# Softmax denominators inverted before they are spread, and one subtraction moved to VectorE

## Chip, core and metric

The kernel runs on one core of a Trainium2 chip. The metric is device time in microseconds (us) of one execution. The engines are TensorE (PE, its weight loads are shown as PEld), VectorE (DVE), ScalarE (ACT), GpSimd (POOL) and SyncE (SP), which issues the DMAs.

## What is computed

A stack of transformer layers over 256 latent and 256 context tokens of 1024 features, all in float32. Four places matter here, all of them softmax attention:

- two layers of the first block, each with 8 query heads of 64 features (grouped, 2 key heads), over 512 keys for a latent token and 256 for a context token;
- a causal attention of 16 heads ("moba"), and a causal attention of 16 heads with compressed keys and queries ("mla"), both over 256 tokens.

```python
s = jnp.einsum("bqhd,bkhd->bhqk", q, k) * scale
p = jax.nn.softmax(s, axis=-1)
out = jnp.einsum("bhqk,bkhd->bqhd", p, v)
```

Between and behind the two causal attentions stand two feed-forward stages (2816 hidden features) with a short convolution, and each attention is followed by an output projection `w_o` of 1024 x 1024.

## The kernel before, in words

**Float32 products in three parts.** Each operand of a large product is split in a rounded part (hi, a cast on ACT) and the rest (lo, `src - hi`). `split` (L130) does this: `S.copy(hi, src)` on ACT and the subtraction on VectorE, unless its last argument names another engine. PE then does hi\*hi, lo\*hi and hi\*lo (`mm3`, L105). Weights come by DMA into `st` (4 buffers), are split into `wh` and `wl` (5 buffers each) and are read by PE; some of the `wl` are made by POOL.

**Softmax without a division of the weights.** For each head PE makes the scores, VectorE takes the maximum, ACT the exponential with the row sum as a by-product (a column of `dn`), PE transposes the weights, ACT or VectorE copies them out of PSUM (`PT`), and PE multiplies them with the values, feature-major, into a bank `pv`. What is still missing is the division by the row sum. The sums are columns (a token is a partition), the values stand as rows (a token is a column), so the inverses must be turned: `inv_rows` (L290) makes from 4 or 8 columns of sums a tile with each inverse 64 times side by side, PE transposes that tile into a bank `tr`, ACT copies the bank to SBUF, and VectorE multiplies `pv` with it.

**Where it is called.** `attend` (L757) calls it for 4 heads at a time, 8 times in the first layer and 4 times in the second; the result goes to `qo` (L800, L801). `out_heads` (L1041) calls it for 8 columns (4 heads by 2 tiles of queries), 4 times in moba and 4 times in mla: the copy on ACT (L1046), the product on VectorE (L1047), and then `split` of the product into `moh`/`mol` or `loh`/`lol`, with the low part on POOL (L1048). These are the operands of the output projection `w_o_proj` (L1050), whose sums go to `h` on VectorE (L1060) and on into the next norm (L982, L983). The tile with the spread inverses is called `t` in `attend` and `rr` in `out_heads`, where it has one buffer.

**Order.** The steps are written in the order of `PLAN` (L46). From it a planner makes one instruction order for each engine before the program runs: it goes through the program with durations that it estimates itself and lets each engine take the foremost instruction that is ready. Each engine then works through its list in that order, whatever the real durations are, and waits at semaphores. `tr`, `sc`, `acc` and `pv` are PSUM banks, two of each.

Of the kernel before, what the change touches and what calls it, by code (L numbers as in the profile page):

```python
# [16 lines left out]
D = 1024  # L17
# [22 lines left out]
# shift 8, scale 8, gate 8  # L40
# [4 lines left out]
# orders of the steps whose results meet only at the end (see the tables `steps`)  # L45
# [11 lines left out]
# pieces of weights whose low parts are worked out by GpSimd (see the keys given to `fetch`)  # L57
# [5 lines left out]
# tile 0, 1: latent tokens; 2, 3: context tokens  # L63
# [5 lines left out]
def tile_two_blocks(ctx: ExitStack, tc: tile.TileContext, A, out, dbg=None):  # L69
# [42 lines left out]
    def stream(pieces, ncol, tiles, sh, sl, tags):  # L112
        """tokens of `tiles` @ a chunk of weights, two k at a time; returns a bank per tile"""
        ps = {t: bank(tag) for t, tag in zip(tiles, tags)}
        for i, w in enumerate(pieces):
            for t in tiles:
                stream_on(ps[t], i, w, ncol, t, sh, sl)
        return ps
# [46 lines left out]
    msk0 = consts.tile([128, 2, 128], F32, name="c_masks")      # 0 / NEG : free > partition, free < partition  # L165
    consts = first.enter_context(tc.tile_pool(name="consts1", bufs=1, side="right", reuse_waits="tile"))

    def rsqrt_into(dst, ss, mean_scale, eps, tmp):
        # dst = (ss * mean_scale + eps) ** -0.5
        n = dst.shape[-1]  # L170
        V.tensor_scalar(tmp, ss, mean_scale, eps, op0=OP.mult, op1=OP.add)
        G.tensor_tensor(dst, tmp, nhalf[:, :n], op=OP.pow)

    # ------------------------------------------------------------------ first block
# [9 lines left out]
    # 512 features of silu(c) @ w_ada + b_ada -> mod[feature, 24, (lat, ctx)]  # L184
    # j < 4: scales of tiles 2j, 2j + 1 of the features and their shifts; then the gates
    def ada_mm(ps, i, st):
        # four quarters of the sum, each in its own columns of the array: they run side by side
        for u in range(2):
            k = 2 * i + u
            r = slice(k % 4 * 32, k % 4 * 32 + 32)  # L190
            mm(ps[r, :], s32[:, k, :], st[u] if type(st) is list else st[:, u * 512:(u + 1) * 512], k < 4, k >= 4)
# [25 lines left out]
    bada = const("b_ada")       # [128, l, 24]  # L217
# [15 lines left out]
    gsec = base.tile([128, 6, 8], F32, name="c_g_sec")      # g_final, norm_mix 0, 1, norm_ffn 0, 1, norm_final  # L233

    def late_consts():
        nc.sync.dma_start(gsec, A["g_sec"])
        late["tri"] = const("tri")          # [128, 2, 128] inclusive prefix / suffix
        late["ropeq"] = const("rope_lat")   # [128, 2 tiles, 2 (cos, sin), 64]
        late["bg"] = const("b_gates")       # [128, l, 16]
        late["gh"] = const("g_head")        # [128, l, 2]  # L240
        late["ends"] = const("ends")        # [128, 2] one in the last / first row
        nc.sync.dma_start(msk0, A["masks"])
        mskp = consts.tile([128, 2, 128], F32, name="mskp")
        G.tensor_scalar(mskp[:, 0], msk0[:, 1], -1.0, None, op0=OP.mult)
        G.tensor_scalar(mskp[:, 1], msk0[:, 0], -1.0, None, op0=OP.mult)
        late["mskp"] = mskp

    class Squares:
        """sum over the features of squares, a tile of 128 features at a time; a column of sums for each tile of tokens"""
# [14 lines left out]
        def add(self, ap, scale=1.0):  # L264
# [10 lines left out]
            if self.k == KT - 1:        # all but the last tile: ahead of it  # L275
                self.ps = bank("tr")
                self.head = self.small("sqh")
                V.tensor_scalar(self.head, self.columns(self.acc, 0), 1.0 / D, self.eps, op0=OP.mult, op1=OP.add)

        def mean(self, dst):  # L280
            """mean of the squares + eps"""
            V.scalar_tensor_tensor(dst, self.columns(self.last, 1), 1.0 / D, self.head, op0=OP.mult, op1=OP.add)
# [7 lines left out]
    def inv_rows(rr, cols):  # L290
        """columns of heads -> rows of 1 / x, a pair of heads in the two halves of the partitions, a pair after the other"""
        n = cols.shape[-1]
        rr = rr[:, :n * 64].rearrange("p (a b) -> p a b", b=64)
        V.reciprocal(rr, cols.unsqueeze(2).to_broadcast([128, n, 64]))  # L294
# [11 lines left out]
    mod_rows = {}       # what is left of the next layer's shifts, scales and gates, and behind which tile  # L306

    def first_layer(l, ncx, x, rc):
        """ncx: context tokens are updated (layer 0) or only read (layer 1)"""
# [8 lines left out]
        # ---- norm  # L318
# [8 lines left out]
        def normed(k, t, r=None):  # L327
# [3 lines left out]
            # the first tile by halves: the products wait for it  # L331
# [12 lines left out]
        gqk = sb.tile([128, 2, 2, 64], F32, name="c_g_qk")      # (q, k), (straight, swapped)  # L344
# [11 lines left out]
        if l == 0:  # L356
            # the first products follow the shifts and scales, two tiles of the features at a time
            def ada_tiles(q):
                """tiles that are not in use yet"""
# [75 lines left out]
        # tables with the gains of q and k folded in  # L435
# [7 lines left out]
        # ---- token-major projections  # L443
# [21 lines left out]
        def rope(dst, src, tab, nh, t, e1=V, e2=V):  # L465
            """dst, src [128, nh, 64]"""
# [11 lines left out]
        # chunk 1: v of the recurrent branch, k and v of the attention  # L478
# [27 lines left out]
        # chunk 3: q of the attention  # L506
# [24 lines left out]
        # chunk 0: k of the recurrent branch and its gates  # L531
# [14 lines left out]
        def gate_stats():  # L546
# [11 lines left out]
            # cumulative sums, their ends (on all partitions and as rows)  # L558
# [45 lines left out]
            V.tensor_tensor(ex[:, 0], mp, Mc, op=OP.subtract)      # inter  # L604
            V.tensor_tensor(ex[:, 1], mp, Me, op=OP.subtract)      # decay of the state
            V.tensor_tensor(ex[:, 2], R, Me, op=OP.subtract)       # weight of a key in the state
# [4 lines left out]
        # chunk 2: q of the recurrent branch, v of the gated mlp  # L611
# [26 lines left out]
        # ---- feature-major gates  # L638
        # a a b b b b c c: the products with the gates land here too
# [17 lines left out]
        # ---- recurrent branch  # L657
# [8 lines left out]
        def scores(c):  # L666
            """heads 0, 2 in one bank, 1, 3 in the other: row tiles of the array run side by side"""
# [6 lines left out]
        HP = [0, 2, 1, 3]       # place of a head in ag  # L674
# [81 lines left out]
        # ---- attention of one tile of queries  # L756
        obs, att = {}, {}  # L757

        def attend(t, i):
            """pair i of the heads"""  # L760
# [4 lines left out]
            if i == 0:  # L765
                # a head: its half holds hi of q, the other half lo
# [26 lines left out]
            # two heads side by side in the columns of the array  # L793
# [15 lines left out]
        def gates(i, q):  # L809
# [3 lines left out]
            if i >= 4:      # bz  # L813
                silu2(gate[:, 2 + (i - 4) * 2 + q, :], ps)
            elif q == 0:    # co; au
# [5 lines left out]
            else:           # cz; az  # L821
# [7 lines left out]
        # gated mlp  # L829
# [20 lines left out]
        # the branches, and products that need none of them in between  # L850
# [14 lines left out]
        if ncx:  # L865
            # what is left of the next layer's shifts, scales and gates
# [33 lines left out]
        if ncx:  # L900
            # they are worked out while the norm is on its way
# [20 lines left out]
        # the next norm: (r^2 * mean((x g)^2) + eps) ** -0.5  # L922
# [15 lines left out]
    def gelu2(dst, ps, tmp):  # L938
        """2 * tanh-gelu(ps); dst and tmp in SBUF"""
# [11 lines left out]
    # ------------------------------------------------------------------ second block  # L951
    consts = ctx.enter_context(tc.tile_pool(name="consts2", bufs=1, reuse_waits="tile"))
    rope2 = const("rope2")      # [128, 2 tiles, (cos, sin), 64]
    rope3 = const("rope3")      # [128, 2 tiles, (cos, sin), 32]
    gqn = const("g_lora")       # [128, 5]: q_norm 3, kv_norm 2
    cw = const("conv")          # [128, l, 22, 4]: taps 0..2, bias
# [9 lines left out]
    class Norm:  # L966
        """next norm of h: hi and lo of h * gain and the sum of squares, as the tiles of h come in"""
# [32 lines left out]
    def scores_of(qT, kT, *heads):  # L1000
        """of heads in different rows of the array: they run side by side"""
# [7 lines left out]
    def weights_of(sb, ps, hd, dn, scale, bufs):  # L1009
        """transposed softmax numerators of a head: [keys, (tile 0, keys 0), (tile 1, keys 0), (tile 1, keys 1)]"""  # L1010
        d0 = hd // 2 * 4 + hd % 2       # pairs of heads, tiles of queries, heads
# [18 lines left out]
    def values_of(PTs, va, g0):  # L1030
        """four heads of P @ v, feature-major: pairs of heads, side by side in the columns of the array"""
# [9 lines left out]
    def out_heads(sb, po, dn, oh, ol, g):  # L1041
        """normalised, hi and lo"""
# [5 lines left out]
        split(oh[:, 2 * g:2 * g + 2, :], ol[:, 2 * g:2 * g + 2, :], o, G)  # L1048
# [95 lines left out]
    def mla(nrm):  # L1144
# [4 lines left out]
        # down projections: 384 of q, then 256 of kv and 32 of the shared key  # L1149
# [10 lines left out]
        def lora_rstd(ps, n, t, dst):  # L1160
            # dst = r * (r^2 * mean(ps^2) + eps) ** -0.5
# [52 lines left out]
        # keys, feature-major  # L1214
# [154 lines left out]
# ---------------------------------------------------------------------- host: layout only  # L1369
def _fp(a):  # L1370
    """[1024, n] -> [128, 8, n]: features on the partitions"""
    return a.reshape(-1, 128, a.shape[-1]).transpose(1, 0, 2)


def _kpack(w):
    """[K, n] -> [128, K/128 * n]"""
    k, n = w.shape
    return w.reshape(k // 128, 128, n).transpose(1, 0, 2).reshape(128, -1)


def _blocks(w, bw=128):
    """[K, N] -> [N/bw, 128, K/128 * bw]"""
# [4 lines left out]
def _pairs(b):  # L1387
    """[2n, 128, m] -> [n, 128, 2m]"""
# [3 lines left out]
def _constants():  # L1392
# [8 lines left out]
    # 2-D rotation of the first block  # L1401
# [78 lines left out]
```

## Time and profile before

| what | before |
| --- | --- |
| time, median of 3 runs | 1162.22 us (1160.79 to 1164.43) |
| span of the profiled execution | 1164.8 us |
| PE busy | 1110.9 us, 95% of the span |
| DVE busy | 765.8 us, 66% |
| ACT busy | 596.9 us, 51% |
| POOL busy | 311.7 us, 27% |
| mean granted TensorE clock | 0.981 |

The profile is that of one execution, and its span, from the first to the last instruction, is 1164.8 us: 0.2% above the median of the timed runs and just above the slowest of them. What lies around the span is not shown. PE works nearly all of the time, so a microsecond of another engine matters where PE waits for it, and only there. The granted clock is 1.0 at 2.4 GHz and 0.5 at 1.2 GHz.

### The profile page before, as it was taken

How to read it: one execution, taken by the hardware profiler on the slowest of the kernel's cores; microseconds unless marked ns; L12 is line 12 of the kernel's file. 1: busy time of each engine (PE TensorE's matmuls, PEld its weight loads, DVE VectorE, ACT ScalarE, POOL GpSimd, SP SyncE). 2: the span in 40 equal slices, each digit the busy share in tenths (PEclk: the TensorE clock that was granted, in tenths of full speed). 3: DMA queues.
4: the chain of work that ended last, by engine and by line, in shares of the span. 5: the costliest groups of instructions: out<-in, count | busy, mean ns of one | idle time of the engine just before them, and what ended most of it. 6: DMA issues, size and time to landing. Idle time of an engine off the chain costs nothing. (4 is left out here: it accounts for less than half of the span.)

```text
span 1164.8 us, 20350 instructions
## 1 busy us (share of the span) xinstructions
PE 1110.9 (95%) x7762; PEld 963.1 (83%) x7762; DVE 765.8 (66%) x1497; ACT 596.9 (51%) x1154; POOL 311.7 (27%) x290
## 2 busy tenths in 40 slices
PE   5899998999899899998999999999999989999997
PEld 2586777687686789887776899999998789999996
DVE  3465555585646666778676777776557877777653
ACT  3435643533434366465456565555447856555541
POOL 3452311131212544424313312221032241222100
PEclk9999998999899899999999999999999999999998
DMA  9523501433742324214443255555644325555561
GB/s 347 200 66 125 177 28 39 142 130 123 259 153 73 101 91 146 74 69 143 162 153 118 82 175 195 184 183 179 182 145 150 135 71 181 185 183 189 175 186 47
DMA packets 52608, 167.29 MB, mean 144 GB/s; under 512 B 6816, under 2 KB 10400, under 8 KB 52512
## 3 DMA queue, kind: packets, MB, share of 16 engines
q1 hardware_dynamic: 52512, 166.01, 42.8%
q8 instruction: 61, 1.00, 0.3%
q14 instruction: 35, 0.29, 0.1%
HBM read 164.41 MB, written 1.05 MB: 142 GB/s over the span
## 5 line engine op out<-in xcount | busy, mean ns | idle before, releaser
L131 ACT CAST wh<-st 128x1024 fp32r<-128x1024 f32 (+4 forms) x272 | 268.5, 992 | 208.9 <-PE acc L100 116.3
L132 DVE TENSOR_TENSOR wl<-st,wh 128x1024 fp32r<-128x1024 f32 (+4 forms) x207 | 244.5, 1183 | 113.3 <-ACT wh L131 108.9
L132 POOL TENSOR_TENSOR wl<-st,wh 128x1024 fp32r<-128x1024 f32 (+4 forms) x65 | 150.9, 2332 | 285.1 <-ACT wh L131 264.5
L100 PE MATMUL acc<-xyh,wh 128*128 128x512 f32 (+1 forms) x320 | 112.5, 352 | 4.3 <-DVE xres L892 2.3
L100 PE MATMUL acc<-xyl,wh 128*128 128x512 f32 (+1 forms) x320 | 111.5, 351 | 2.6 <-DVE xyl L132 2.6
L100 PE MATMUL acc<-xyh,wl 128*128 128x512 f32 (+1 forms) x320 | 111.4, 349 | 0.0
L100 PE MATMUL acc<-wh,xyh 128*128 128x512 f32 (+1 forms) x256 | 97.6, 382 | 6.4 <-DVE t L474 3.3
L100 PE MATMUL sc<-hh,wl 128*128 128x256 f32 x352 | 99.0, 281 | 0.0
L100 PE MATMUL sc<-hl,wh 128*128 128x256 f32 x352 | 99.0, 281 | 0.0
L100 PE MATMUL acc<-hl,wh 128*128 128x256 f32 x352 | 99.0, 281 | 0.0
L100 PE MATMUL acc<-ah,wh 128*128 128x256 f32 x352 | 99.0, 281 | 0.0
L100 PE MATMUL acc<-al,wh 128*128 128x256 f32 x352 | 99.0, 281 | 0.0
L100 PE MATMUL acc<-ah,wl 128*128 128x256 f32 x352 | 98.9, 281 | 0.0
L100 PE MATMUL sc<-hh,wh 128*128 128x256 f32 x352 | 98.9, 281 | 0.0
L100 PE MATMUL acc<-hh,wh 128*128 128x256 f32 x352 | 98.8, 281 | 0.0
L100 PE MATMUL acc<-hh,wl 128*128 128x256 f32 x352 | 98.8, 281 | 0.0
L100 PE MATMUL acc<-wh,xyl 128*128 128x512 f32 (+1 forms) x256 | 96.0, 375 | 0.0
L100 PE MATMUL acc<-wl,xyh 128*128 128x512 f32 (+1 forms) x256 | 95.3, 376 | 0.0
L100 PEld LDWEIGHTS acc<-xyh,wh 128*128 128x128 f32 x320 | 62.2, 194 | 13.5 <-issue 2.8
L100 PEld LDWEIGHTS acc<-xyl,wh 128*128 128x128 f32 x320 | 62.0, 194 | 10.8 <-DVE xyl L132 3.1
L100 PEld LDWEIGHTS acc<-xyh,wl 128*128 128x128 f32 x320 | 62.0, 194 | 7.6
L100 PEld LDWEIGHTS sc<-hl,wh 128*128 128x128 f32 x352 | 66.4, 189 | 0.0
(458 smaller groups left out, 2746.2 us busy)
## 6 DMA issues: line engine op xcount, KB each, us to landing
st<-w_gu SPq DMA_DIRECT2D x88, 512.0 KB, 3.8
st<-w_dn SPq DMA_DIRECT2D x32, 512.0 KB, 3.5
st<-w_in_t SPq DMA_DIRECT2D x24, 512.0 KB, 3.9
st<-w_in_f SPq DMA_DIRECT2D x24, 512.0 KB, 4.7
st<-a_w_qkv SPq DMA_DIRECT2D x24, 512.0 KB, 3.4
st<-w_ada SPq DMA_DIRECT2D x20, 512.0 KB, 3.9
st<-w_out SPq DMA_DIRECT2D x16, 512.0 KB, 4.4
st<-w_dn SPq DMA_DIRECT2D x16, 384.0 KB, 3.3
```

The lines of the kernel that those rows point to most:

```text
L100: last_mm[0] = PE.matmul(o, lhsT, rhs, start=start, stop=stop).ins
L131: S.copy(hi, src)
L132: (lo_eng or V).tensor_tensor(lo, src, hi.bitcast(F32), op=OP.subtract)
```

## The change

`inv_rows` no longer takes 1/x of the spread columns (256 or 512 elements in each partition). It takes 1/x of the 4 or 8 sums in place, and a copy on VectorE spreads the result. And in `out_heads` the low part is subtracted on VectorE, where POOL did it. All else in the diff is removed comments and docstrings.

```diff
     def inv_rows(rr, cols):
...
         n = cols.shape[-1]
         rr = rr[:, :n * 64].rearrange("p (a b) -> p a b", b=64)
-        V.reciprocal(rr, cols.unsqueeze(2).to_broadcast([128, n, 64]))
+        V.reciprocal(cols, cols)
+        V.tensor_copy(rr, cols.unsqueeze(2).to_broadcast([128, n, 64]))
         pt = bank("tr")
...
     def out_heads(sb, po, dn, oh, ol, g):
...
         V.tensor_tensor(of, po, of, op=OP.mult)
-        split(oh[:, 2 * g:2 * g + 2, :], ol[:, 2 * g:2 * g + 2, :], o, G)
+        split(oh[:, 2 * g:2 * g + 2, :], ol[:, 2 * g:2 * g + 2, :], o)
```

## Rows read from the trace of the kernel before

**Rows 1.** The page, part 1: busy time, share of the span, instructions.

```profile
PE 1110.9 (95%) x7762; PEld 963.1 (83%) x7762; DVE 765.8 (66%) x1497; ACT 596.9 (51%) x1154; POOL 311.7 (27%) x290
```

**Rows 2.** Groups by line and shape, VectorE: count | busy us, mean ns | idle before.

```profile
L294 DVE RECIPROCAL t<-dn 128x256 f32<-128x256 f32 x12 | 21.0, 1750 | 14.4 <-ACT P L787 14.4
L294 DVE RECIPROCAL rr<-mdn 128x512 f32<-128x512 f32 x4 | 13.4, 3350 | 1.4 <-ACT sm L1019 1.1 <-PE tr L156 0.3
...
L341 DVE TENSOR_TENSOR xyl<-t,xyh 128x512 fp32r<-128x512 f32 x15 | 10.3, 689 | 0.3
...
L714 DVE TENSOR_TENSOR hsum<-n,den 128x256 f32<-128x256 f32 x6 | 2.5, 421 | 0.1
...
L710 DVE RECIPROCAL den<-den 128x4 f32<-128x4 f32 x12 | 2.1, 174 | 0.3
```

**Rows 3.** Line 294 alone: who waited for its results (us, times).

```profile
  PE tr L156: 2.0, 2
```

**Rows 4.** Timeline of PE, end of moba: start, us, instruction [idle before <-releaser].

```profile
639.84 1.04 PE L156 MATMUL tr<-c_ident,rr 128*128 128x128 f32 x4 [1.34 <-DVE nb L1014]
...
650.29 0.87 PE L100 MATMUL pv<-PT,mva 128*64 128x128 f32 x10 [0.29 <-DVE PT L1025]
...
654.03 0.39 PE L100 MATMUL acc<-mol,wh 128*128 128x256 f32 x1 [0.52 <-POOL gn L1321]
```

**Rows 5.** Timelines of VectorE, ACT and POOL in the same stretch.

```profile
636.35 3.35 DVE L294 RECIPROCAL rr<-mdn 128x512 f32<-128x512 f32 x1
...
639.61 0.23 DVE L1014 CUSTOM_DVE_ANT_0 sm<-sc,cmask 128x128 f32<-128x128 f32 x1
...
639.76 0.69 DVE L1047 TENSOR_TENSOR ov<-pv,ov 128x512 f32<-128x512 f32 x1
...
645.88 3.35 DVE L294 RECIPROCAL rr<-mdn 128x512 f32<-128x512 f32 x1 [0.26 <-PE tr L156]
...
636.94 0.57 ACT L1046 COPY ov<-tr 128x512 f32<-128x512 f32 x1
...
641.40 0.62 ACT L131 CAST moh<-ov 128x512 fp32r<-128x512 f32 x1
...
652.69 1.28 POOL L132 TENSOR_TENSOR mol<-ov,moh 128x512 fp32r<-128x512 f32 x1 [0.91 <-ACT moh L131]
```

**Rows 6.** Timeline of PE, end of mla.

```profile
935.95 0.66 PE L156 MATMUL tr<-c_ident,rr 128*128 128x128 f32 x4 [1.01 <-DVE rr L294]
...
937.63 0.55 PE L156 MATMUL tr<-c_ident,sm 128*128 128x128 f32 x3 [0.70 <-ACT ov L1046]
...
940.20 1.02 PE L156 MATMUL tr<-c_ident,rr 128*128 128x128 f32 x4 [1.01 <-DVE rr L294]
```

**Rows 7.** Timelines of VectorE and ACT in the same stretch.

```profile
932.54 3.35 DVE L294 RECIPROCAL rr<-ldn 128x512 f32<-128x512 f32 x1
...
936.70 3.35 DVE L294 RECIPROCAL rr<-ldn 128x512 f32<-128x512 f32 x1 [0.26 <-PE tr L156]
...
936.47 0.62 ACT L131 CAST loh<-ov 128x512 fp32r<-128x512 f32 x1 [2.04 <-DVE ov L1047]
936.99 0.58 ACT L1046 COPY ov<-tr 128x512 f32<-128x512 f32 x1
```

**Rows 8.** Busy time by stretch: us, engines (instructions), granted clock, DMA share, GB/s.

```profile
639.90:643.30 3.40, 3.40 (x28) 3.00 (x28) 3.40 (x9) 2.86 (x10) 1.20 (x1) 0.50 0.02 5
...
940.30:943.70 3.40, 3.40 (x19) 2.74 (x20) 1.45 (x3) 1.38 (x3) 1.27 (x1) 0.50 0.00 0
...
312.20:319.00 6.80, 5.83 (x14) 4.59 (x15) 4.22 (x7) 1.60 (x2) 0.29 (x1) 0.50 0.53 161
```

**Rows 9.** Waits of PE from 95 to 320 us: total us, times, longest.

```profile
PE acc L100 <- DVE xyl L132: 2.6, 1, 2.6
```

**Rows 10.** Timelines of VectorE and POOL just behind moba.

```profile
657.25 3.98 DVE L983 SCALAR_TENSOR_TENSOR hl<-hres,c_g_sec,hh 128x256 fp32r<-128x256 f32 x2 [1.54 <-ACT hh L982]
...
656.00 4.95 POOL L132 TENSOR_TENSOR wl<-st,wh 128x1024 fp32r<-128x1024 f32 x2 [1.91 <-ACT wh L131]
```

## The prediction

> **What bounds the kernel now.** I read the page first: PE is busy for 1110.9 of 1164.8 us [rows 1], so it is PE's list of instructions that sets the time, and only the 53.9 us in which PE stands still, or works at half clock, can be won or added to. VectorE is busy for 765.8 us [rows 1]; what is taken from it is worth nothing by itself. Next I looked the touched line up. Its 20 reciprocals take 21.0 us in `attend` and 13.4 us in each of moba and mla, 47.8 us in all [rows 2], yet the view of that line finds only two waits of PE's array for its results, 2.0 us together [rows 3]. So nearly all of the 47.8 us lies beside PE's work. But that view credits a wait to one releaser, and a reciprocal also holds up what is queued behind it on VectorE. So third I went through PE's timeline at the 20 places for idle time, and through VectorE's at the same moments. In the two layers of the first block I found no idle time of PE that a reciprocal ends. At the ends of moba (636 to 654 us) and mla (931 to 942 us), where four `out_heads` stand close together and little other work is left for PE, I found six stalls that hang on the touched instructions:
>
> - 1.34 us before the transposes of `rr` at 639.84 [rows 4]. The row names another releaser, but the reciprocal that those transposes read runs from 636.35 to 639.70 [rows 5]; it ends 0.14 us before they start.
> - 0.29 us before the value products at 650.29 [rows 4]: they wait for a copy of `PT`, which VectorE reaches only after the reciprocal from 645.88 to 649.23 [rows 5] and a product.
> - 0.52 us before the projection's products at 654.03 [rows 4]: they need the last `mol`, on POOL from 652.69 to 653.97 [rows 5]; the `gn` in the row is POOL's next small instruction.
> - 1.01 us twice, at 935.95 and 940.20 [rows 6], behind the reciprocals from 932.54 to 935.89 and from 936.70 to 940.05 [rows 7].
> - 0.70 us at 937.63 [rows 6]: transposes wait for a bank `tr` that ACT empties at 936.99, held up by the cast before it, which waited 2.04 us for a product on VectorE queued behind the reciprocal [rows 7].
>
> Last I looked at the clock. From 639.90 to 643.30 and from 940.30 to 943.70 it was granted at 0.50, 1.2 GHz, with PE busy all the time [rows 8]. Each stretch begins just after the stalls named: PE had stood still for 1.34 us up to 639.84 in one, and for 1.01, 0.70 and 1.01 us within the 5 us before 940.20 in the other.
>
> **The change part by part.** *The reciprocal.* 1/x of 4 columns exists already: 0.174 us [rows 2]. I take 0.18 us for 8 as well. The copy that spreads is not in the trace in this form. It can't be shorter than the 0.174 us of the smallest operation. From above, the nearest rows are a product with a spread operand of 4 columns, 0.421 us for 256 elements, and a two-input subtraction of 512 elements, 0.689 us [rows 2]. I take the upper ends, since they have the shape. With 4 columns: 0.17 + 0.42 = 0.59 instead of 1.75 us, 1.16 less; with 8: 0.18 + 0.69 = 0.87 instead of 3.35 us, 2.48 less. VectorE loses 12 x 1.16 + 8 x 2.48 = 33.8 us.
>
> The Trainium skill, "VectorE: DVE Perf Modes", section "The perf-mode tier table (the rule you actually need)", lets a float32 copy inside SBUF run at twice the rate of a two-input operation. By that the copies would be some 0.15 to 0.25 us shorter (an estimate from that page); the sum below would be the same, since no stall is that short of vanishing.
>
> *The wait that is added.* The copy waits for the reciprocal on its own engine, and behind it is queued what was queued behind the old reciprocal. `den` is used in the same way and its chain shows no idle time over 0.3 us in 12 [rows 2], so I price it at 0.03 us. The old wait for `rr`, which has one buffer, now falls on the copy alone: the reciprocal of 8 columns can go ahead of it.
>
> *The low part.* VectorE takes on 8 subtractions of 128x512, 0.69 us each [rows 2], 5.5 us. POOL loses 8 x 1.28 us [rows 5]. For the last group of each attention, this shortens the way to the projection by 0.59 us, more than the 0.52 us that PE waits there. For the other groups it adds a wait: the subtraction needs ACT's cast, and VectorE's products, maxima and copies of `PT` stand behind it. In moba the cast of the first group ended at 642.02, 1.57 us after its product ended at 640.45 [rows 5]; in the seven other groups the cast begins at once and takes 0.62 us [rows 7]. So this costs VectorE between 0 (the planner puts ready work in between) and 1.57 + 7 x 0.62 = 5.9 us, which its 33.8 us pay for. I take 1 us, hidden by PE's work.
>
> *What PE gets back.* With 2.48 us less before it, each of the reciprocal's stalls is covered: 1.34, 0.29 and 0.52 us in moba; 1.01 and 1.01 us in mla. Of the 0.70 us ACT's own copy stays: the transposes before it end at 936.61, and 0.58 us for the copy [rows 7] leads to 937.2 where PE would be ready at about 936.9, so 0.3 stays and 0.4 goes. That is 2.15 + 2.42 = 4.6 us. What is late next is ACT (casts of `moh`, `loh`) and VectorE's copies of `PT`. By moving every row of the moba end to the left I find the last `mol` ready 0.2 us before PE asks for it: no new stall, but little room.
>
> *The clock.* If the stalls go, I see nothing that would bring the two stretches at half clock. A stretch of 3.40 us of work at half clock would be 1.70 us at full clock. Four transposes took 1.04 us in it and 0.66 us outside [rows 4, 6], which is less than half as fast would give, 2.15 us for the 3.40. I take 1.5 us saved for each, 3.0 in all (between 1.25 and 1.70 each).
>
> *The first block.* The 12 shorter reciprocals (13.9 us) and 0 of PE's time: price 0, hidden by PE's own products. The 5.1 us of POOL's low parts in each attention go where POOL had nothing else to do.
>
> Sum: 4.6 + 3.0 = 7.6 us of the profiled execution, whose span of 1164.8 would be 1157.2. Behind both places PE runs a dense list (its products, not a time of day, lead the feed-forward stages), so the shift reaches the end. The timed median is 0.2% lower than that span; the same 7.6 us from 1162.2 gives 1154.6 us.
>
> **The rivals.** *The stalls go, the clock does not come back.* PE does light work there (transposes, products over 64 rows), and other short stalls stay. For: 0.3 us stays before 937.63. Against: each stretch follows stalls of over 1 us. Time: 1162.2 - 4.6 = 1157.6 us, or 1156.1 with one of the two.
>
> *The next bound takes the place of the old one.* VectorE waits for ACT's cast with the subtraction at the head of its queue, and PE for the `PT` copies behind it: the 5.9 us above, of which some 4 reach PE and keep part of the stalls and the clock with them. For: the 1.57 us in moba. Against: VectorE has 2.48 us more room at each place. Time: about 1159 to 1161 us.
>
> *The new copy and subtraction are slowed by POOL.* Behind moba two `hl` take 3.98 us while POOL makes weights [rows 10], against 0.69 us for an operation of twice their size when POOL is still [rows 2]. The old reciprocal kept its 3.35 us everywhere. The Trainium skill, "GPSIMD Engine Reference", section "8. Key points", says the same of operations with two SBUF inputs and of fast copies, and so speaks against the exchange; the `hl` rows bear it out. Price: up to about 2 us per copy, which is what the exchange saves. But at the ends of moba and mla POOL does nothing but the low parts that leave it. In the first block it may happen, hidden. Time: as forecast, within 1 us; I give it no chance of its own.
>
> *Slower: the planner's order.* Its lists come from its own estimates, and the edit changes 28 instructions and adds 20. VectorE's list has the product at 639.76 behind the maximum of a later head at 639.61, though ACT had its operand ready at 637.51 [rows 5]; a planner that gave the reciprocal before them 3.35 us, to 639.70, would have seen it ready and put it first. So I think that it takes the reciprocal for about 1 us or less, and the new lists should look like the old. But one changed place in the first block can bring a stall like that of 2.6 us [rows 9] with its stretch of 6.80 us at half clock behind it [rows 8], some 2.6 + 3.0 us. One takes most of the gain (1160.2), two make it 1166 us: it decides from the second on. That the change doesn't do what it says (a copy as slow as the reciprocal) I exclude: 0.42 us for a spread operand is in the rows.
>
> **How the numbers follow.** Forecast 1154.6 us: 0.43, with its own range 1152 to 1156. Clock stays, wholly or in part: 0.20 (1156 to 1158). Next bound: 0.12 (1159 to 1161). Order: 0.18, of which one stall or about even 0.09 (1159 to 1165), and slower 0.09 (1166 and more). More gain than forecast, from orders that happen to be better: 0.07 (1149 to 1152). The bound of 0.3%, 3.5 us, is about what a measurement of this kernel can tell from no change: faster means below 1158.7 us, slower above 1165.7. Faster: 0.43 + 0.20 + 0.07 + 0.02 of the next bound = 0.72. Slower: 0.09. Same: the rest, 0.19. The range, 1151 to 1162.5, leaves out the slower case and the better half of the lucky one.
>
> **What would show it.** Right: at line 295 of the new kernel 20 copies of 0.2 to 0.7 us, and reciprocals of about 0.2 us; no wait of PE over 0.3 us between the scores of the last heads and the projection in moba and mla; clock 1.00 there; the remaining stalls of PE, in the first block above all, where they were. Wrong: idle time on VectorE before the subtractions of `mol` and `lol` with PE waiting for `PT`; new stalls of over 1 us in the first block; stretches at half clock in either attention without a stall before them.

## The result and the profile after

The changed kernel took 1154.66 us (median; 1153.81 to 1155.10), the kernel before 1162.24 us beside it. The ratio is 0.9935, with a 95% interval from 0.9921 to 0.9949. A second comparison of the same pair, with more runs (e5 below), gave 0.9957 (0.9943 to 0.9971). So the changed kernel is faster by some 0.4 to 0.7%, 5 to 8 us, and the 1154.6 us forecast was met. That the first median lies within 0.1 us of it is luck, and inside the sum some terms were too large and others too small, as the following sections show.

The page of the kernel after, part 1, in the columns of [rows 1]:

```profile
PE 1102.5 (96%) x7762; PEld 956.8 (83%) x7762; DVE 737.8 (64%) x1525; ACT 597.8 (52%) x1154; POOL 301.8 (26%) x282
```

VectorE has 28.0 us less to do and POOL 9.9 us less; the prediction's terms gave 28.3 and 10.2. For VectorE the closeness is luck in part: the copies were 3.6 us cheaper than taken, and three of them, beside work of POOL, took 3.8 us longer than the others (see the rivals below). The touched lines of the kernel after, by shape (count: shortest, median and longest in ns, first and last start), first the reciprocals, then the copies, then the subtraction that is now on VectorE:

```profile
L294 DVE RECIPROCAL dn<-dn x12: 168/178/180, 101.9 to 504.6; 128x4 f32<-128x4 f32 x12
L294 DVE RECIPROCAL mdn<-mdn x4: 194/203/204, 598.4 to 637.3; 128x8 f32<-128x8 f32 x4
...
L295 DVE COPY t<-dn x12: 284/294/2407, 102.1 to 505.2; 128x256 f32<-128x256 f32 x12
...
L295 DVE COPY rr<-mdn x4: 423/425/427, 598.6 to 637.6; 128x512 f32<-128x512 f32 x4
...
L132 DVE TENSOR_TENSOR mol<-ov,moh x4: 685/691/692, 636.1 to 646.0; 128x512 fp32r<-128x512 f32 x4
```

A group of 8 columns now costs 0.20 + 0.43 us where [rows 2] has 3.35, one of 4 columns 0.18 + 0.29 where it has 1.75. Neither line has an instruction of PE waiting for it, where [rows 3] had two.

TensorE's timeline at the end of moba in the kernel after (start, us, instruction, idle before and its releaser), to set against [rows 4]:

```profile
634.10 0.66 PE L156 MATMUL tr<-c_ident,rr 128*128 128x128 f32 x4
...
643.67 0.87 PE L100 MATMUL pv<-PT,mva 128*64 128x128 f32 x10
646.04 0.38 PE L100 MATMUL acc<-moh,wh 128*128 128x256 f32 x1 [1.50 <-ACT moh L131]
```

The three stalls of [rows 4] are gone, 1.34, 0.29 and 0.52 us. In their place stands one that was not there: 1.50 us before the products of the last group. At the end of mla, PE's timeline has one stall over 0.3 us left of the three in [rows 6]:

```profile
928.77 0.55 PE L156 MATMUL tr<-c_ident,sm 128*128 128x128 f32 x3 [0.40 <-ACT ov L1047]
```

The clock at both places, busy time by stretch in the columns of [rows 8]:

```profile
633.00:640.00 7.00, 6.83 (x70) 5.79 (x71) 5.63 (x17) 6.00 (x18) 0.00 (x0) 1.00 0.01 2
640.00:647.00 7.00, 5.50 (x46) 4.62 (x45) 2.54 (x4) 1.23 (x3) 0.17 (x3) 1.00 0.00 0
...
924.00:931.00 7.00, 6.60 (x68) 5.38 (x66) 4.42 (x12) 4.49 (x12) 0.00 (x0) 1.00 0.00 0
```

It was granted in full in these stretches; the two at 0.50 in moba and mla of [rows 8] are gone.

To see where the 7 us came from, I cut the span of each profile at two landmarks of PE's timeline: the first scores of moba (`sc<-mKT,mQT`) and the first scores of mla (`sc<-K,Q`). These are the rows in the kernel before, then after:

```profile
581.59 0.49 PE L100 MATMUL sc<-mKT,mQT 64*128 64x128 f32 x4
889.98 1.06 PE L100 MATMUL sc<-K,Q 96*128 96x128 f32 x4
```

```profile
577.26 0.49 PE L100 MATMUL sc<-mKT,mQT 64*128 64x128 f32 x4
882.79 1.06 PE L100 MATMUL sc<-K,Q 96*128 96x128 f32 x4
```

This gives three parts in us; the table has every kernel that was run, since the experiments are read from it:

```
                                first block   moba part   mla part   span
before                             581.59       308.39     274.82   1164.8
after                              577.26       305.53     270.53   1153.3
e1 reciprocal and copy only        579.72       306.93     270.69   1157.3
e2 low part only                   577.09       308.54     273.82   1159.4
e3 new line for 8 columns only     576.55       305.42     270.66   1152.6
e4 new line for 4 columns only     575.58       308.50     273.53   1157.6
e5 the change again                582.49       305.53     270.89   1158.9
e6 six more copies into rr         576.64       311.07     281.94   1169.6
e7 no copy                         575.93       305.61     271.95   1153.5
e8 four banks                      577.92       305.70     270.01   1153.6
e9 last heads earlier              575.00       304.09     271.73   1150.8
e10 last heads one step earlier    578.14       304.79     270.82   1153.7
e11 six copies beside              577.08       313.59     273.13   1163.8
```

The change takes 2.86 us from the moba part and 3.9 to 4.3 us from the mla part, about 7 us. A narrower cut says where: from the first scores to the last product of the attention's output projection PE takes 91.75 us in moba and 76.35 us in mla before, 88.94 and 72.05 after (88.90 and 72.17 in e5). Behind that product the rest of the moba part is 216.6 us in all four of before, after, e4 and e5, and the rest of the mla part 198.5 to 198.7 us.

The first block is another matter: the two profiles of the one changed program (after and e5) differ there by 5.2 us, and before, e2 and e3, in which PE's list is the same there, by up to 5.0. No difference between two kernels in the first block is put down to a cause below, and what is said of the other parts rests on their own columns.

### The profile page after: what moved, and what is told of

It is laid out like the page before. It is cut to its first block, busy times and chain, and to the rows that moved or that the text cites. A ratio compares the mean times of both kernels' runs of the same rounds, so it can differ in the third digit from the quotient of the medians.

```text
span 1153.3 us, 20355 instructions
## 1 busy us (share of the span) xinstructions
PE 1102.5 (96%) x7762; PEld 956.8 (83%) x7762; DVE 737.8 (64%) x1525; ACT 597.8 (52%) x1154; POOL 301.8 (26%) x282
## 4 chain that ended last, share of the span: by engine, by line
PE 81%; DVE 7%; issue 7%; ACT 2%; DMA 2%; SPq 0%; POOL 0%; POOLq 0%; DVEq 0%; ACTq 0%
PE acc L100 49%; PE sc L100 19%; PE pv L100 6%; PE tr L156 6%; PE tr L100 1%; ACT wh L131 1%; DVE hl L984 1%; DMA st<-w_ada 1%; DMA st<-w_out 1%; DMA xres<-xc 1%; DVE wl L132 1%; DVE sqa L271 0%; DVE xyl L132 0%; DVE xres L402 0%; DVE t L475 0%
```

## The experiments

**Which edit carries it.** Four kernels split the change: the two edits, and the two shapes of the touched line.

*e1: the new reciprocal and copy, low parts on POOL as before.*

```
-        split(oh[:, 2 * g:2 * g + 2, :], ol[:, 2 * g:2 * g + 2, :], o)
+        split(oh[:, 2 * g:2 * g + 2, :], ol[:, 2 * g:2 * g + 2, :], o, G)
```

> The short reciprocals and the copy everywhere, the low parts back on POOL. Theory (the stalls at the ends of moba and mla were made by the length of the 8 long reciprocals): 1155 to 1156 us, within 1 us of the whole change, since the low part was worth at most the 0.52 us before the last mol in moba. Rival (VectorE instead of POOL for the low part is what shortens the way to the projection, 0.6 us in each group): 1157 to 1159 us.

Measured: 1155.81 us, ratio 0.9957 (0.9940 to 0.9973). The mla part is as short as with the whole change, 270.69 us; the moba part is 1.40 us longer, 306.93. PE's waits between 640 and 655 us in e1 (waiter, releaser: us, times, longest):

```profile
PE acc L100 <- ACT moh L131: 1.5, 1, 1.5
PE acc L100 <- POOL gn L1322: 0.6, 1, 0.6
```

The first is the new stall of the whole change too. The second is the last `mol` on POOL, 0.6 us, as the prediction had read it in [rows 4] (0.52). Behind it stands a stretch at half clock, from 650.1 to 653.5 us:

```profile
650.10:653.50 3.40, 3.40 (x16) 3.40 (x17) 0.85 (x2) 2.35 (x4) 1.17 (x1) 0.50 0.01 2
```

So nearly all of the gain is the reciprocal's, and the subtraction adds 1.4 us in moba: the wait for POOL and what follows it. That is read from the parts; the timed ratio is that of the whole change in e5.

*e2: the old long reciprocal, low parts on VectorE.*

```
-        V.reciprocal(cols, cols)
-        V.tensor_copy(rr, cols.unsqueeze(2).to_broadcast([128, n, 64]))
+        V.reciprocal(rr, cols.unsqueeze(2).to_broadcast([128, n, 64]))
```

> The long reciprocals as before, only the low parts on VectorE. Theory (length of the reciprocals): 1161.5 to 1163 us, as before or a little slower, since eight subtractions of 0.69 us stand behind reciprocals of 3.35 us on the same engine. Rival (the low part carries a share of the gain): 1158 to 1160 us.

Measured: 1161.82 us, ratio 1.0005 (0.9993 to 1.0018): no gain and no loss. PE's waits from 630 to 650 and from 920 to 940 us in e2:

```profile
PE tr L156 <- DVE nb L1014: 1.3, 1, 1.3
PE tr L156 <- DVE rr L294: 1.3, 2, 0.9
```

```profile
PE tr L156 <- DVE rr L294: 2.0, 1, 2.0
```

The subtraction is worth something only once the reciprocal is out of the way. In moba the waits for POOL and for `PT` that the kernel before has (0.52 and 0.29 us) are gone, but two waits for `rr` of 1.3 us together stand in their place, behind reciprocals of 3.35 us on the same engine. The moba part is as long as before, 308.54 us.

*e3 and e4: the new line for 8 columns only (moba and mla, low parts on VectorE), and for 4 columns only (first block, low parts on POOL).*

```
+        if n == 8:            # e3; in e4: n == 4
+            V.reciprocal(cols, cols)
+            V.tensor_copy(rr, cols.unsqueeze(2).to_broadcast([128, n, 64]))
+        else:
+            V.reciprocal(rr, cols.unsqueeze(2).to_broadcast([128, n, 64]))
```

> Short reciprocals in out_heads alone, low parts on VectorE; attend in the first block keeps its 12 reciprocals of 1.75 us, so PE's list there is that of the kernel before. Theory (all of the gain lies at the ends of moba and mla): 1154.5 to 1156 us. Rival (the first block gives a part of it, by shorter waits or by fewer stretches at half clock): 1157 to 1159 us.

> Short reciprocals in attend alone; out_heads as before, low parts on POOL. Theory (nothing of PE's time hangs on the 12 reciprocals of 4 columns): 1161 to 1163 us. Rival (the first block gives a part, as its stretch in the two profiles, 4.3 us shorter, would say): 1157 to 1159 us.

Measured: e3 1156.08 us, ratio 0.9963 (0.9949 to 0.9977); e4 1160.22 us, 0.9994 (0.9984 to 1.0005). e3 lies just above the range of its theory; e4 lies below that of its theory and above that of its rival, but the kernel before took 1161.16 us beside it, and the interval of its ratio holds 1. So shortening the 12 reciprocals of the first block, 21.0 us of VectorE's time [rows 2], is worth nothing that can be measured, as predicted, and the 8 of moba and mla carry the gain.

e4 also shows what the clock was worth. In moba and mla PE's list is that of the kernel before, instruction for instruction; the stalls are there, and no stretch at half clock. PE's timeline at the end of moba in e4:

```profile
633.82 0.63 PE L156 MATMUL tr<-c_ident,rr 128*128 128x128 f32 x4 [1.34 <-DVE nb L1018]
...
637.01 0.39 PE L100 MATMUL acc<-mol,wh 128*128 128x256 f32 x1 [0.33 <-POOL mol L132]
...
639.11 0.66 PE L156 MATMUL tr<-c_ident,rr 128*128 128x128 f32 x4 [0.88 <-DVE rr L298]
```

Busy time by stretch there, clock 1.00:

```profile
632.00:640.00 8.00, 5.37 (x49) 4.21 (x49) 7.74 (x14) 3.72 (x12) 1.28 (x1) 1.00 0.01 2
```

The stall of 1.34 us is that of [rows 4]. In the kernel before half clock followed it; here full clock, and two waits more, 0.33 and 0.88 us, which the kernel before does not have there. The moba part is 308.50 us without the stretch and 308.39 with it. At half clock PE had only reached later what it would have waited for anyway: VectorE, busy 7.74 of these 8.00 us, set the pace. In mla the stretch did cost something: 274.82 us with it against 273.53 without, 1.3 us. That the stretches are absent in e4 at all, behind the same stalls, also means that they need not be there in every timed run of the kernel before.

*e5: the changed kernel a second time.*

> The changed kernel once more, beside the next three and on their chip, since the first block was seen to differ by up to 6 us between profiles of the same instruction lists. Theory (the stages from moba's scores to the end of mla's projection give the whole gain, 7.1 us between the two profiles): 0.6% below the kernel before, 6 to 8 us. Rival (the parts measured alone add up to 5 us, and the rest was luck of the first block): 0.4%, 4 to 5.5 us.

Measured: 1155.21 us, ratio 0.9957 (0.9943 to 0.9971). By time this is the second theory's 0.4%, though the interval reaches to 0.57%, 6.6 us. By the parts it is the first theory's: moba and mla together take 576.4 us where the kernel before has 583.2, 6.8 us less. So the parts show where the gain is made, and the median leaves its size open between 5 and 8 us. Among the 12 runs those with a lower granted clock are on the whole the longer ones: 0.984 at 1160.70 us, 0.990 at 1153.33.

**Where the limit lies now.** *e7: without the copy.* Each head's column is spread by TensorE itself, as the stationary operand of a small product.

```
-        V.tensor_copy(rr, cols.unsqueeze(2).to_broadcast([128, n, 64]))
-            transpose(pt[:, p * 128:(p + 1) * 128], ...)
+            for u in range(2):
+                mm(pt[u * 64:u * 64 + 64, p * 128:(p + 1) * 128],
+                   cols[:, 2 * p + u:2 * p + u + 1].to_broadcast([128, 64]), ident)
```

> The spreading copy is gone: PE multiplies the unit matrix with each column of inverses, read 64 times over, two products of 64 columns where one transpose of 128 stood. VectorE loses 8 x 0.43 and 12 x 0.29 us, PE gets 40 transposes replaced by 80 smaller products. Theory (no time of PE hangs on VectorE here any more): as the changed kernel, within 1 us. Rival (VectorE still ends the waits at the ends of moba and mla): 1.5 to 3 us less than the changed kernel.

Measured: 1156.05 us, ratio 0.9957 (0.9940 to 0.9974). The new stall in moba shrinks to 0.3 us:

```profile
PE acc L100 <- ACT moh L131: 0.3, 1, 0.3
```

But PE pays for the products that take the copy's place itself. In moba there are 64, four for each of the 16 transposes that they replace, and they keep it busy for 4.5 us, where the 16 transposes took 2.5 us in the kernel after:

```profile
L100 PE MATMUL tr<-c_ident,mdn 128*64 128x128 f32 x64 | 4.5, 277 | 0.0
```

The moba part comes out as long as with the copy, 305.61 us. So the time is the first theory's, but not for its reason: the stall did shrink, and the products cost what that gave. What is taken from an engine with room and given to the one that sets the time has to save more than it costs there.

*e8: four PSUM banks instead of two for the output projection behind moba and mla.*

```
-                ps = bank("acc")
+                ps = bank(("acc", "sc")[q])
```

> The changed kernel with the sums of the output projections going to the banks acc and sc in turn, so that four of them can be open at once. In the changed kernel PE waits 1.50 us for the last cast of moh with nothing else to do, and 0.42, 0.32 and 0.24 us for a bank to be emptied. Theory (PE now lacks work that does not need the last group of heads): those waits go, 2 to 2.5 us less than the changed kernel. Rival (the chain from the value products over VectorE and ACT to the last moh ends the stage whatever PE has to do): within 0.5 us of it.

Measured: 1155.23 us, ratio 0.9954 (0.9937 to 0.9971). The waits in the projection vanish, 1.50 us for the last `moh` and 0.42 for a bank; waits at the norm behind it and at the first sums of the feed-forward stage, between 677 and 679 us, take their place. All waits of PE from 640 to 680 us in e8:

```profile
PE acc L100 <- DVE gn L1323: 1.4, 1, 1.4
PE tr L156 <- POOL nrc L287: 0.9, 1, 0.9
```

The moba part is 305.70 us, as long as after, so the banks don't end that stage. That the chain from the last group through the norm does, as the rival has it, is argued from these two waits; no run shortens that chain.

*e9 and e10: the order of the last heads.* In the kernel after, the value products of the last group stand at 643.67 us behind the products of the first three groups, though the last copy of `PT` that they read ended at 641.2. VectorE's timeline there:

```profile
640.67 0.55 DVE L1026 COPY PT<-tr 128x384 f32<-128x384 f32 x1
644.64 0.69 DVE L1048 TENSOR_TENSOR ov<-pv,ov 128x512 f32<-128x512 f32 x1 [3.43 <-PE pv L100]
646.02 0.69 DVE L132 TENSOR_TENSOR mol<-ov,moh 128x512 fp32r<-128x512 f32 x1 [0.68 <-ACT moh L131]
```

VectorE waits 3.43 us for PE, and then PE waits 1.50 us for the chain behind it, product and cast, with nothing else in its list. e9 and e10 move the scores of the last heads forward in the written order of moba:

```
-    ... | h10 o0 v1 v2 h12 h13 o1 o2 h14 h15 v3 o3"
+    ... | h10 o0 v1 v2 h12 h13 h14 h15 o1 o2 v3 o3"     # e9
+    ... | h10 o0 v1 v2 h12 h13 o1 h14 h15 v3 o2 o3"     # e10
```

> The changed kernel with two entries of the written order of the first part's attention moved: the scores of the last two heads, h14 and h15, ahead of the outputs of groups 1 and 2 (o1, o2), so that the value products of the last group stand ahead of the products of the output projection that they stood behind. Theory 1: the wait of 1.50 us that the changed kernel has before the products of the last group is made by its list, in which those value products come at 643.67 us though their last operand was there at 641.2. It goes, the part from the first scores to the second attention's first scores is 304.0 us long where it was 305.5, and the time is 1.5 us less than the changed kernel's (0.9944 of the kernel before where the change was 0.9957). Theory 2: the chain copy, multiply, cast, subtract of VectorE and ScalarE is what ends last there; with the heads earlier the first groups' outputs come later, the wait stands before another group, and the part is 305 to 307 us long.

> As the run before, but the last two heads and the value products v3 stand behind the output of group 1 and ahead of that of group 2. Theory 1: the wait of 1.50 us goes or falls under 0.5, because the value products of the last group come earlier than 643.67 us against the products of the projection; the part is 304.0 to 304.5 us long. Theory 2: the wait moves to another group and the part stays at 305 to 307 us.

Measured: e9 1152.65 us, ratio 0.9925 (0.9906 to 0.9945), the best of all kernels here; e10 1154.94 us, 0.9949 (0.9930 to 0.9969). In e9 the stall is gone. PE's longest waits from 626 to 650 us:

```profile
PE pv L100 <- DVE ov L1048: 0.6, 2, 0.4
PE tr L156 <- DVE rr L295: 0.5, 1, 0.5
```

Its moba part is 304.09 us, 1.44 less than after, as the first theory had it (304.0). e10 leaves 0.38 us of the stall, and its part is 304.79 us, a little more than expected. So the new stall was the list's doing. The intervals of e9 and of the change overlap; what carries the verdict is the part, and it stands for 1.4 us: the rest by which e9's median lies lower has no cause shown here.

**How much room VectorE has.** *e6: six more copies of the same sums into the same `rr`, in moba and mla.*

```
         V.tensor_copy(rr, cols.unsqueeze(2).to_broadcast([128, n, 64]))
+        if n == 8:
+            for i in range(6):
+                V.tensor_copy(rr, cols.unsqueeze(2).to_broadcast([128, n, 64]))
```

> The changed kernel with the spreading copy made seven times instead of once in out_heads, so that VectorE is held up about as long as by the old reciprocal (7 x 0.43 us and 0.20 against 3.35). Theory (it is the time on VectorE ahead of the transposes that makes the stalls): most of the gain is lost, 1160 to 1162 us, stalls of about 1 us before the transposes of rr. Rival (the planner had taken the reciprocal for short; it sees the copies and puts other work there): 1155 to 1158 us, no stall over 0.5 us before those transposes.

Measured: 1170.49 us, ratio 1.0089 (1.0068 to 1.0110): slower than the kernel before by 9.5 us, which no theory had. The largest stall stands at the end of mla. VectorE's timeline, then PE's:

```profile
934.66 0.43 DVE L295 COPY rr<-ldn 128x512 f32<-128x512 f32 x1 [1.51 <-PE tr L156]
...
935.47 0.69 DVE L1051 TENSOR_TENSOR ov<-pv,ov 128x512 f32<-128x512 f32 x1
...
936.86 0.69 DVE L132 TENSOR_TENSOR lol<-ov,loh 128x512 fp32r<-128x512 f32 x1
937.46 1.34 DVE L298 COPY rr<-ldn 128x512 f32<-128x512 f32 x3
```

```profile
934.03 0.60 PE L156 MATMUL tr<-c_ident,rr 128*128 128x128 f32 x4
938.95 0.63 PE L156 MATMUL tr<-c_ident,rr 128*128 128x128 f32 x4 [4.33 <-DVE rr L298]
```

`rr` has one buffer. The first copy waits until the transposes of the group before have read it (934.66), the seventh ends at 938.80, with a product and a subtraction in between, and the next transposes start at 938.95. The seven pieces were spread over 4.1 us, where the one reciprocal takes 3.35. PE then worked at half clock from 939.9 to 946.7 us. What the stall and this stretch each cost was not measured apart.

*e11: the same six copies, into a tile that nobody reads.*

```
         pt = inv_rows(sb.tile([128, 512], F32, name="rr2", bufs=1), ...)
+        spare = sb.tile([128, 8, 64], F32, name="spare", bufs=1)
+        for i in range(6):
+            V.tensor_copy(spare, dn[:, 8 * g:8 * g + 8].unsqueeze(2).to_broadcast([128, 8, 64]))
```

> The changed kernel with six more copies of the same sums and size for each of the eight groups of heads, as in the run with six more copies, but written into a tile of its own that nobody reads, so that no transpose waits for them: VectorE has the same 2.6 us more to do in each group, and the chain from reciprocal to transposes is as short as in the change. Theory 1, the chain decides: what made 1170.5 us was that the transposes waited behind seven copies into one buffer; these copies go where VectorE is idle, and the time is that of the change to 3 us more (1155 to 1158). Theory 2, VectorE's load decides: its backlog of 2.6 us in each group delays scores, multiplies and subtractions alike, and the time is 1165 to 1171 again. Between the two, waits of TensorE for multiplies or subtractions show how much the backlog costs without the chain.

Measured: 1165.79 us, ratio 1.0046 (1.0030 to 1.0062). By its number the second theory, VectorE's load. But the sum of the load can't be the whole reason: per group it is 0.20 + 7 x 0.43 + 0.69 = 3.9 us, and e2, with 3.35 + 0.69 = 4.0 us, took 1161.82. The mla part shows what the removed chain was worth, 273.13 against 281.94 us in e6. The moba part is 8.06 us longer than after, and PE's one long wait in it stands at one place. VectorE and POOL in e11, then PE:

```profile
625.31 4.30 DVE L1047 COPY spare<-mdn 128x512 f32<-128x512 f32 x5
```

```profile
626.05 2.35 POOL L132 TENSOR_TENSOR wl<-st,wh 128x1024 fp32r<-128x1024 f32 x1 [3.76 <-ACT wh L131]
```

```profile
630.22 1.28 PE L100 MATMUL sc<-mKT,mQT 64*128 64x128 f32 x4 [2.70 <-DVE nb L1017]
```

Five copies of 0.43 us took 4.30 instead of some 2.2 us, since one of them ran beside POOL's subtraction. The line of all 24 shows it as the longest, 2.45 us:

```profile
L1047 DVE COPY spare<-mdn x24: 418/426/2453, 598.8 to 650.8; 128x512 f32<-128x512 f32 x24
```

The next scores' reductions stood behind it, PE waited 2.70 us, and then came 13.70 us at half clock with PE busy in all of it:

```profile
630.60:644.30 13.70, 13.70 (x59) 9.22 (x60) 8.19 (x34) 7.35 (x27) 0.00 (x0) 0.50 0.05 18
```

So the price of added work depended on where it stood: here, ahead of the reductions that the scores wait for, and beside POOL. What the stall and the stretch behind it each cost was not measured apart.

## Why the prediction came out right, and where its steps were off

**What held.** The bound: PE's list, with the ends of moba and mla as the places. Behind both, PE's dense list takes as long as before (216.6 and 198.5 us), so the shift does reach the end. The view of the touched line credited 2.0 us to it [rows 3], yet some 7 us came back; going through PE's idle time at the places and asking what was queued behind the reciprocal found the rest. The first block: price 0 (e4). Of the six stalls that were named five went wholly, and the sixth in part. In mla the stalls and the stretch at half clock were taken for 2.42 + 1.5 = 3.9 us, and 3.9 to 4.3 came; e4 splits it in 1.3 for the clock and the rest, 2.6 to 3.0, for the stalls. Of the 0.70 us, 0.3 was to stay; 0.40 did. The last `mol` on VectorE was right as well: e1 has the wait of 0.6 us on POOL, the change hasn't.

**"No new stall, but little room" failed.** This is the step that moved every row of the moba end to the left and found the last `mol` ready in time. It moved the rows of the old list. But the planner made a new one, in which the last value products stand behind the products of three groups, and the last `moh`, not `mol`, is late: 1.50 us. The sign that the prediction gave for itself, no wait of PE over 0.3 us at these places, is broken there. e9 gave 1.44 us of it back by order alone. The same holds for "the new lists should look like the old". The two lists of PE do differ, at both ends and in the first block. The row from which the planner's estimate was inferred (a product put behind a maximum) could bear that the estimate for the reciprocal was short, not that nothing else would move. No run has the new line with the old lists, so what else the new orders gave or took was not measured.

**The clock term in moba was mis-sized.** 1.5 us was taken for the stretch behind 639.84, on the ground that four transposes took 1.04 us instead of 0.66. This is what PE's work took longer, not what the end came later by: in e4 the stretch is absent, and the part is as long (308.50 against 308.39 us), because VectorE's chain set the pace. In mla, where PE was not so held, it was 1.3 us. This is its worth while the long reciprocals are there. No run has the stalls gone and these stretches kept; behind the short reciprocals of e1 a stretch of 3.40 us cost some 0.8 us, the 1.40 us of its moba part less the wait of 0.6 (an estimate).

**The stalls in moba were worth more than their waits.** They were taken for 2.15 us. With the order of e9, which has no stall of 1.50 us, the moba part gives 308.39 - 304.09 = 4.30 us for stalls and clock together, more than the 2.15 + 1.5 forecast. All of it lies in one stretch of PE's list, from the transposes of the first group's `rr` to the first products of the next bank of the output projection (`acc<-moh,wh`). Busy time by stretch in the columns of [rows 8], in the kernel before, e4, the kernel after and e9:

```profile
635.48:655.29 19.81, 17.55 (x134) 14.02 (x132) 15.31 (x23) 9.63 (x28) 5.22 (x7) 0.91 0.02 6
...
629.46:649.27 19.81, 16.31 (x134) 12.71 (x132) 15.32 (x23) 9.58 (x28) 5.23 (x7) 1.00 0.02 7
...
631.14:648.02 16.88, 15.15 (x135) 12.55 (x133) 9.59 (x28) 9.53 (x28) 0.17 (x3) 1.00 0.02 7
...
628.88:644.31 15.43, 14.09 (x134) 12.12 (x133) 9.77 (x28) 9.80 (x28) 0.17 (x3) 1.00 0.02 8
```

From e4 to e9, both at full clock, the stretch loses 4.38 us. PE's idle time falls from 3.50 to 1.34 us, and its busy time by 2.2 us for the same number of instructions. These 2.2 us can be put down to waits as well. In a dense row a product of 0.28 us starts every 0.12 us, as here in the kernel after:

```profile
639.69 0.28 PE L100 MATMUL acc<-moh,wh 128*128 128x256 f32 x1
639.81 0.28 PE L100 MATMUL acc<-moh,wl 128*128 128x256 f32 x1
```

Where the list is held up, the row of the last product still runs its 0.28 us, so up to 0.16 us of each hold counts as busy. In e4, 34 instructions of the stretch start more than 0.15 us after the one before, in e9 20: 14 holds fewer, of 0.16 us each, would be 2.2 us (an estimate). A sum over the listed waits leaves these short holds out.

**The sum.** moba gave 2.86 us for the 3.65 forecast, since the new stall took 1.44 of the 4.30 us, and mla 3.9 to 4.3 for 3.92: some 7 us for 7.6. In moba the size came near because the errors partly cancel.

**The copies' prices.** I took the upper ends, 0.42 and 0.69 us; they took 0.29 and 0.43. The lower values are those that the sentence on the Trainium skill, "VectorE: DVE Perf Modes", section "The perf-mode tier table (the rule you actually need)", pointed to: a float32 copy in SBUF at twice the rate of a two-input operation. Here the copies were 0.13 and 0.26 us shorter, near the 0.15 to 0.25 us estimated there. It made no difference to the sum, as said there. The bound from below, 0.174 us, was not the smallest operation of the trace (`DVE_READ_ACCUMULATOR2_ANT` takes 0.08 us), but nothing hung on it.

**The rivals.** *The clock does not come back*: it came back, in both profiles of the change; but the stretches are absent in e4 too, with the stalls there. *The next bound takes its place*: partly, with ScalarE's cast of `moh`, but by the order of the list and not by a limit of ScalarE or VectorE (e9). *POOL slows the copies*: it happens, and was rightly held harmless here. Three of the 12 copies of the first block took 0.6, 1.7 and 2.4 us; the longest, on VectorE and POOL in the kernel after:

```profile
495.71 2.41 DVE L295 COPY t<-dn 128x256 f32<-128x256 f32 x1
```

```profile
495.59 2.38 POOL L132 TENSOR_TENSOR wl<-st,wh 128x1024 fp32r<-128x1024 f32 x1
```

The copy ends 0.15 us behind POOL's subtraction. The Trainium skill, "GPSIMD Engine Reference", section "8. Key points", names contention of GpSimd with VectorE's instructions in a two-port mode or with two SBUF inputs, and the trace agrees. e11 shows the same 2.4 us at a place where it isn't hidden. *The planner's order, slower*: the lists changed, and the price was 1.4 us in moba, not a stall in the first block.

## What to carry to other kernels

Take a long operation off an engine for what stands behind it in its queue at the places where the bounding engine runs out of other work; what it costs everywhere else, here the 21.0 us of reciprocals in the first block, is worth nothing. When a planner makes the lists, look at the new lists before counting on the old rows: one group of products in another place took a third of the gain in moba, and moving two entries of the written order gave it back. Short holds of PE did not show as idle time here, so compare the length of the whole stretch and not only its listed waits. Work added to an engine with a third of its time free still made the kernel slower than before by 4 to 10 us, because it stood ahead of what others waited for.

## What the runs showed of the hardware

The granted clock behind one and the same stall differs between executions of one program. In the kernel after and in e5, the same program, PE waits 3.3 us for `t` and goes on with the same product. The row of PE and the stretch behind it, first after, then e5:

```profile
399.17 0.47 PE L100 MATMUL acc<-wh,xyh 128*128 128x512 f32 x1 [3.33 <-DVE t L475]
...
396.00:403.00 7.00, 3.83 (x17) 3.14 (x18) 7.00 (x19) 0.99 (x3) 5.96 (x5) 1.00 0.34 99
```

```profile
401.37 0.77 PE L100 MATMUL acc<-wh,xyh 128*128 128x512 f32 x1 [3.32 <-DVE t L475]
...
400.50:407.30 6.80, 5.93 (x14) 4.76 (x15) 6.07 (x15) 0.00 (x0) 6.15 (x4) 0.50 0.40 119
```

The product took 0.47 us in one and 0.77 in the other. The stall of 1.34 us in moba is another case: half clock behind it in the kernel before, full clock in e4, with the same list. So the prediction's tie of half clock to the stalls, read from one profile, is no property of the stall alone. What else decides it stays open. Such stretches do account for what the first block differs by between these two profiles: e5 has two more such stretches there than the kernel after, of 6.8 us each (at 274.2 and 400.5 us), and PE is busy there for 545.5 us against 539.7, 5.7 us more where the block is 5.2 us longer.

A copy on VectorE was stretched from 0.43 to 2.45 us beside one subtraction of POOL, and ended 0.3 us behind it; the old reciprocal kept its 3.34 us beside such a subtraction too (from 916.72 us in the kernel before, with POOL busy from 917.53 to 919.88).
